# Fifteen added TensorE products between the first modulation units, and h's last low part on VectorE

## The chip, the cores and the metric

The kernel runs on one core of a Trainium2 chip. The metric is the device time of one execution in microseconds. The core has five engines, each with its own queue of instructions in a fixed order: TensorE (PE; PEld is its loading of the stationary operand), VectorE (DVE), ScalarE (ACT), GpSimd (POOL) and SyncE (SP), whose queue issues most of the transfers. The engines wait for one another through semaphores. Products on TensorE are written to banks of PSUM, from which ScalarE or VectorE copies them out.

## The reference

One layer of a streaming encoder is computed for two groups of tokens that share the weights: 256 tokens of a prompt and 8 sequences of 16 tokens. Cut to the part that the change touches:

```python
mod = silu(c) @ w_ada + b_ada            # per sequence, 6 x 1024 columns
sh1, sc1, g1, sh2, sc2, g2 = split(mod, 6)
h = rmsnorm(x, norm1_w) * (1 + sc1) + sh1
P = h @ w_in                             # RWKV-7 | sparse attention and indexer | two gates
```

After that come an RWKV-7 branch, a sparse attention branch, a gated mix with a residual, a second modulated norm and PEER, a mixture of 16,384 single-row experts of which each token picks 8 x 16. Everything is float32; a product has to keep nearly float32 accuracy.

## The kernel before

**High and low parts.** Most products are not made in float32 directly. A tile is split into a high part (`hi`, a copy in the type float32r, made on ScalarE by `hilo`, L230) and a low part (`lo = src - hi`, made on VectorE or GpSimd, L234), and hi*hi + hi*lo + lo*hi are added up in one bank. For weights these parts are `wh` and `wl`; for h they are `LTh` and `LTl`, each of 128 partitions x 8 chunks x 384 tokens (columns 0 to 127 are the sample tokens, 128 to 383 the prompt's).

**The front.** `front_x` loads x in three tiles of 128 tokens, norms them and transposes them on TensorE into `xT` (the `fx` rows). `front_h` then goes over the eight chunks of h in four steps of two, c = 0, 2, 4, 6. Step c calls `mod_unit` for unit c // 2 (shift) and unit c // 2 + 4 (scale), and turns two chunks of `xT` into h and its two parts. The high part of the samples is made on ScalarE (L485) and that of the prompt on VectorE (L486); the low part of the samples on VectorE (L487, 128 x 256), that of the prompt on GpSimd (L488, 128 x 512).

**A modulation unit** has 256 columns of `w_ada`. Its weights come in two slices of 512 KB, each into one of the four buffers `w` of the pool `stream`, from which the weights of `w_in` come too; a transfer waits until the buffer it takes has been read. A slice makes four float32 products, 32 rows x 256 columns, side by side in the array's four column groups (`mm<-w,cst`). After both slices ScalarE copies the bank (`mr`, L392), two small products with `sel` transpose it and add up its four parts (`bx<-cfirst,mr`), and VectorE adds the bias (`scT`, L397). From `scT` comes `h1A` (L404).

**What follows** is `w_in` by units of columns: wa, wb, wg (RWKV's low-rank inputs), two gate units, the indexer, and then, by the string ORDER, RWKV pairs, attention quarters, gate units and the remaining modulation units in turn. The product of a unit with h runs over h's eight chunks in `tposp` or `natp` and lands in one of two banks `mm`; ScalarE copies it out (`pt`, L502 and L503).

**What sets the order.** Within an engine the instructions don't stand as the program's text has them: a scheduler simulates a timeline with its own costs and fills each queue. An edit at one place can therefore move rows of all later stages. `d<-zero` rows clear scratch in memory, `rt` rows on GpSimd make the rotary tables (L343 to L352), `expb` and `ob` are constants of later stages; all three stand among the front's rows. The bank tag `dx` has two buffers, which stages behind the front use.

Of the kernel before, what the change touches and what calls it, by code (L numbers as in the profile page):

```python
# [18 lines left out]
OP = mybir.AluOpType  # L19
# [8 lines left out]
NT = 384  # L28
# [167 lines left out]
class K:  # L196
# [186 lines left out]
    def mod_unit(self, u):  # L383

        nc = self.nc
        p = self.ps([128, 256], tag="mm")
        for h in range(2):
            w = self.raw(self.I["w_ada"][:, u, h * 4:h * 4 + 4])
            for g in range(4):
                self.mm(p[32 * g:32 * g + 32], self.st[:, h * 4 + g], w[:, g], start=(h == 0), stop=(h == 1), tp=(0, 32 * g))  # L390
        mr = self.t([128, 256], tag="mr", bufs=2, pool=self.fill)
        nc.scalar.activation(mr, p, AF.Copy)  # L392
        if u < 8:
            q = self.ps([128, 2, 9], tag="bx")
            for c in range(2):
                self.mm(q[:, c], mr[:, c * 128:(c + 1) * 128], self.c["sel"])
            nc.vector.tensor_tensor(self.scT[:, u // 4, (u % 4) * 2:(u % 4) * 2 + 2], q,  # L397
                                    self.bcol[:, 2 * u:2 * u + 2].unsqueeze(2).to_broadcast([128, 2, 9]), op=OP.add)
        else:
            nc.sync.dma_start(self.modd[:, u * 256:(u + 1) * 256], mr)  # L400
# [62 lines left out]
    def front_h(self):  # L463

        nc = self.nc
        hi = self.t([128, 8, NT], F32R, tag="LTh", pool=self.hpool)
        lo = self.t([128, 8, NT], F32R, tag="LTl", pool=self.hpool)
        self.LT = (hi, lo)
        self.h1B = self.scT[:, 0]
        self.h1A = self.pool.tile([128, 8, 9], F32, name="h1A")  # L470
        h = self.xT
        for c in range(0, 8, 2):
            cs = slice(c, c + 2)
            self.mod_unit(c // 2)
            self.mod_unit(c // 2 + 4)
            self.mod_cols(cs)
            hs = h[:, cs, 0:128]
            o = hs.rearrange("p c (b t) -> p c b t", t=16)
            bc = lambda a: a[:, cs, :8].unsqueeze(3).to_broadcast([128, 2, 8, 16])
            nc.vector.tensor_tensor(o, o, bc(self.h1A), op=OP.mult)  # L480
            nc.vector.tensor_tensor(o, o, bc(self.h1B), op=OP.add)
            for cc in (c, c + 1):
                hp = h[:, cc, 128:NT]
                nc.scalar.activation(hp, hp, AF.Identity, scale=self.h1A[:, cc, 8:9], bias=self.h1B[:, cc, 8:9])
            nc.scalar.activation(hi[:, cs, 0:128], hs, AF.Copy)  # L485
            nc.vector.tensor_copy(hi[:, cs, 128:NT], h[:, cs, 128:NT])  # L486
            nc.vector.tensor_tensor(lo[:, cs, 0:128], hs, hi[:, cs, 0:128], op=OP.subtract)  # L487
            nc.gpsimd.tensor_tensor(lo[:, cs, 128:NT], h[:, cs, 128:NT], hi[:, cs, 128:NT], op=OP.subtract)  # L488


    def shifted(self, name, ch, tag, bufs=2):
# [1263 lines left out]
```

## Time and profile before

| | us |
|---|---|
| three runs: lowest, median, highest | 1762.54, 1763.51, 1766.21 |
| the profiled execution, whole | 1759.49 |
| its span, first to last instruction | 1757.7 |
| busy in the span: PE, DVE, ACT, POOL | 1679.5, 1353.6, 747.5, 550.5 |
| mean granted TensorE clock | 0.981 |

All rows shown below come from the profiled execution, in microseconds from the start of its span. A row of the timeline reads: start, length, engine, line, operation, what is written <- what is read, shapes, how many of them, and in brackets the idle time before it and what ended it. A row of the waits reads: who waited for whom, us in total, how often, the longest. A group's row ends with busy time, mean ns of one, and idle time before. SPq is the queue of SyncE that issues transfers. Ends of products on TensorE are modelled, and products overlap, so that the spacing of two starts says more than a length.

### The profile page before, as it was taken

The page shows a single profiled execution, that of the slowest core. Times are in us where ns is not written, and L with a number is a line of the kernel's source. Part 1 is how long each engine was busy: PE and PEld are TensorE (multiplying, and loading weights), DVE is VectorE, ACT ScalarE, POOL GpSimd, SP SyncE. Part 2 cuts the span into 40 slices and gives each one's busy share as a digit, 9 for nine tenths or more (in the row PEclk, how much of TensorE's full clock was granted, in tenths as well). Part 3 has the DMA queues.
Part 4 walks back from the last instruction along what each step waited for, and adds up shares of the span by engine and source line. Part 5 has one row for each costly group of instructions (what it writes and reads, how often), then busy time and mean ns, then how long its engine had stood idle before and what let it go on. Part 6 is the DMA issues. An engine that isn't in the chain of part 4 may idle for free.

```text
span 1757.7 us, 33129 instructions
## 1 busy us (share of the span) xinstructions
PE 1679.5 (96%) x12392; PEld 1410.2 (80%) x12392; DVE 1353.6 (77%) x2907; ACT 747.5 (43%) x1666; POOL 550.5 (31%) x616
## 2 busy tenths in 40 slices
PE   6999899999999999999998999999999999999998
PEld 4988788777888877899887889999976667767766
DVE  4448878778867765556999998899957778778787
ACT  4533343334342333335323255578853433443344
POOL 2433343333333421024032233342243224323232
PEclk8999899999999999999999999999999999999999
DMA  8543662555365365765488999997569999999996
GB/s 305 161 123 101 187 194 68 145 166 174 94 197 161 94 207 189 246 193 171 144 334 313 358 333 366 397 340 238 179 251 381 348 346 376 375 349 391 349 379 216
DMA packets 172537, 436.71 MB, mean 248 GB/s; under 512 B 46036, under 2 KB 86100, under 8 KB 155992
## 3 DMA queue, kind: packets, MB, share of 16 engines
q1 hardware_dynamic: 153944, 300.36, 50.8%
q0 software_dynamic: 18432, 134.23, 19.7%
q8 instruction: 98, 1.61, 0.4%
q14 instruction: 63, 0.52, 0.1%
HBM read 403.23 MB, written 31.30 MB: 247 GB/s over the span
## 4 chain that ended last, share of the span: by engine, by line
PE 55%; DVE 19%; DMA 11%; issue 8%; ACT 3%; POOL 2%; SPq 1%; DVEq 0%; POOLq 0%; ACTq 0%
PE mm L226 21%; PE fx L226 10%; PE dx L226 10%; PE cp L226 6%; PE bx L226 6%; DMA raw<-in_puv,pe 3%; DVE wl L234 3%; DVE raw L1580 2%; DVE acc L1586 2%; DMA w<-in_puT 2%; DMA w<-in_pv 2%; ACT wh L230 1%; DMA w<-in_w_in 1%; DVE TX L698 1%; DMA NL<-d 1%
## 5 line engine op out<-in xcount | busy, mean ns | idle before, releaser
L234 DVE TENSOR_TENSOR wl<-w,wh 128x1024 fp32r<-128x1024 f32 (+1 forms) x276 | 345.8, 1260 | 109.0 <-ACT wh L230 71.3
L230 ACT ACTIVATE wh<-w 128x1024 fp32r<-128x1024 f32 (+1 forms) x284 | 296.6, 1050 | 163.7 <-PE mm L226 74.3
L1573 POOL DMA_INDIRECT raw<-in_puv,pe x128 | 173.6, 1356 | 423.4 <-PE dx L226 155.4
L226 PE MATMUL fx<-h2h,wl 128*128 128x256 f32 x704 | 200.1, 285 | 8.2 <-DVE wl L234 8.0
L226 PE MATMUL fx<-h2h,wh 128*128 128x256 f32 x704 | 200.6, 285 | 1.4 <-ACT wh L230 1.1
L226 PE MATMUL fx<-h2l,wh 128*128 128x256 f32 x704 | 197.4, 281 | 0.0
L1586 DVE SCALAR_TENSOR_TENSOR acc<-raw,dots,acc 128x1024 f32<-128x1024 f32 x127 | 166.1, 1308 | 14.8 <-ACT dots L1582 14.8
L1580 DVE SCALAR_TENSOR_TENSOR raw<-raw,sh 128x1024 f32<-128x1024 f32 x128 | 158.9, 1241 | 14.0 <-DMA raw<-in_puv,pe 13.8
L226 PEld LDWEIGHTS fx<-h2h,wl 128*128 128x128 f32 x704 | 132.7, 189 | 12.3 <-DVE wl L234 11.5
L226 PEld LDWEIGHTS fx<-h2h,wh 128*128 128x128 f32 x704 | 132.6, 188 | 6.4 <-ACT wh L230 3.6
L226 PEld LDWEIGHTS fx<-h2l,wh 128*128 128x128 f32 x704 | 132.9, 189 | 1.6 <-issue 1.1
L226 PE MATMUL mm<-LTh,wh 128*128 128x384 f32 (+2 forms) x352 | 123.4, 351 | 1.4 <-ACT wh L230 0.8
L226 PE MATMUL mm<-LTl,wh 128*128 128x384 f32 (+2 forms) x352 | 123.1, 350 | 0.9 <-POOL LTl L488 0.9
L226 PE MATMUL mm<-LTh,wl 128*128 128x384 f32 (+2 forms) x352 | 122.4, 348 | 0.0
L226 PE MATMUL mm<-h2f,w 128*128 128x256 f32 x448 | 104.0, 385 | 0.0
L226 PE MATMUL mm<-wh,LTh 128*128 128x256 f32 x336 | 100.3, 299 | 2.9 <-ACT qx L888 2.9
L1581 ACT ACTIVATE dots<-dots 128x1 f32<-128x1 f32 x128 | 25.6, 200 | 177.0 <-DVE raw L1580 176.5
L226 PE MATMUL mm<-wl,LTh 128*128 128x256 f32 x336 | 99.4, 296 | 0.0
L226 PE MATMUL mm<-wh,LTl 128*128 128x256 f32 x336 | 98.6, 293 | 0.0
L226 PEld LDWEIGHTS mm<-h2f,w 128*128 128x128 f32 x448 | 85.0, 192 | 12.2 <-issue 0.2
L226 PE MATMUL fx<-h2f,w 128*128 128x256 f32 x320 | 73.8, 383 | 0.0
L226 PEld LDWEIGHTS mm<-LTh,wh 128*128 128x128 f32 (+2 forms) x352 | 66.5, 189 | 7.1 <-issue 3.0
(577 smaller groups left out, 4235.0 us busy)
## 6 DMA issues: line engine op xcount, KB each, us to landing
w<-in_puT SPq DMA_DIRECT2D x128, 512.0 KB, 7.1
w<-in_pv SPq DMA_DIRECT2D x128, 512.0 KB, 6.6
w<-in_w_in SPq DMA_DIRECT2D x70, 512.0 KB, 4.5
w<-in_w_ada SPq DMA_DIRECT2D x48, 512.0 KB, 4.8
cKT<-in_cKT SPq DMA_DIRECT2D x32, 256.0 KB, 4.3
cV<-in_cV SPq DMA_DIRECT2D x32, 256.0 KB, 4.5
w<-in_w_pq SPq DMA_DIRECT2D x16, 512.0 KB, 4.2
d<-wst SPq DMA_DIRECT2D x8, 832.0 KB, 4.3
```

Of the source, the lines that this page charges most:

```text
L226: return self.nc.tensor.matmul(out, l, r, start=start, stop=stop, skip_group_check=True, **kw)
L230: self.nc.scalar.activation(hi, src, AF.Copy)
L234: (self.nc.vector if eng == "v" else self.nc.gpsimd).tensor_tensor(lo, src, hi, op=OP.subtract)
L698: nc.vector.tensor_tensor(X[:, :t, :t], T[:, :t, :t].rearrange("p s c -> p c s"), NL[:, :t, t].unsqueeze(1).to_broadcast([48, t, t]), op=O ...
L1573: d = nc.gpsimd.indirect_dma_start(out=bass.AP(tensor=u.tensor, offset=u.offset, ap=[u.ap[0], [1, 2048]]), out_offset=None, in_=self.I["puv"],
L1580: nc.vector.scalar_tensor_tensor(u, u, 1.0, h2, op0=OP.mult, op1=OP.mult, accum_out=dot)
L1581: nc.scalar.activation(dot, dot, AF.Gelu_apprx_tanh)
L1586: nc.vector.scalar_tensor_tensor(acc, v, dot, acc, op0=OP.mult, op1=OP.add)
```

## The change

Behind the four products of a slice, in units 0 to 7, TensorE makes one more product: the identity as stationary operand times the slice's last quarter (128 x 128 by 128 x 256, float32), into a bank `wake` that nothing reads. The last slice of unit 7 is left out, so there are fifteen. The bank is one of the two `dx` buffers, taken once ahead of the loop. In the last step (c = 6) the prompt's low part is made on VectorE and no more on GpSimd.

```diff
--- before.py
+++ after.py
@@ -388,6 +388,8 @@
             w = self.raw(self.I["w_ada"][:, u, h * 4:h * 4 + 4])
             for g in range(4):
                 self.mm(p[32 * g:32 * g + 32], self.st[:, h * 4 + g], w[:, g], start=(h == 0), stop=(h == 1), tp=(0, 32 * g))
+            if u < 8 and (u, h) != (7, 1):
+                self.mm(self.wake, self.ident, w[:, 3])
         mr = self.t([128, 256], tag="mr", bufs=2, pool=self.fill)
         nc.scalar.activation(mr, p, AF.Copy)
         if u < 8:
@@ -469,6 +471,7 @@
         self.h1B = self.scT[:, 0]
         self.h1A = self.pool.tile([128, 8, 9], F32, name="h1A")
         h = self.xT
+        self.wake = self.ps([128, 256], tag="dx")
         for c in range(0, 8, 2):
             cs = slice(c, c + 2)
             self.mod_unit(c // 2)
@@ -485,7 +488,7 @@
             nc.scalar.activation(hi[:, cs, 0:128], hs, AF.Copy)
             nc.vector.tensor_copy(hi[:, cs, 128:NT], h[:, cs, 128:NT])
             nc.vector.tensor_tensor(lo[:, cs, 0:128], hs, hi[:, cs, 0:128], op=OP.subtract)
-            nc.gpsimd.tensor_tensor(lo[:, cs, 128:NT], h[:, cs, 128:NT], hi[:, cs, 128:NT], op=OP.subtract)
+            (nc.vector if c == 6 else nc.gpsimd).tensor_tensor(lo[:, cs, 128:NT], h[:, cs, 128:NT], hi[:, cs, 128:NT], op=OP.subtract)
 
 
     def shifted(self, name, ch, tag, bufs=2):
```

The lines of the changed kernel are two or three further down from there on. How the queues stand now is shown at three places; a number behind a name tells one buffer of a tile from another, and such numbers differ between the two programs throughout.

TensorE, the first two units. `mm` are the products of a slice, `dx` the added ones, `fx` transposes of the second x tile, `bx` the sel products. Before:

```order
L226 MATMUL mm_174<-w_175,cst 32x256 x4
L226 MATMUL mm_174<-w_181,cst 32x256 x4
L460 MATMUL fx_138<-cfirst,xn_131 128x128 x4
L460 MATMUL fx_144<-cfirst,xn_131 128x128 x4
L226 MATMUL mm_193<-w_194,cst 32x256 x4
L226 MATMUL bx_189<-cfirst,mr_187 128x9 x2
L226 MATMUL mm_193<-w_200,cst 32x256 x4
L226 MATMUL mm_221<-w_222,cst 32x256 x4
```

And with the change:

```order
L226 MATMUL mm_175<-w_176,cst 32x256 x4
L226 MATMUL dx_174<-w_176,cfirst 128x256
L226 MATMUL mm_175<-w_183,cst 32x256 x4
L226 MATMUL dx_174<-w_183,cfirst 128x256
L462 MATMUL fx_138<-cfirst,xn_131 128x128 x4
L462 MATMUL fx_144<-cfirst,xn_131 128x128 x4
L226 MATMUL mm_196<-w_197,cst 32x256 x4
L226 MATMUL dx_174<-w_197,cfirst 128x256
L226 MATMUL mm_196<-w_204,cst 32x256 x3
L226 MATMUL bx_192<-cfirst,mr_190 128x9 x2
L226 MATMUL mm_196<-w_204,cst 32x256
L226 MATMUL dx_174<-w_204,cfirst 128x256
```

Each slice `w` is now read by a fifth product that stands directly behind its four; the transposes of the second x tile stand behind two of these.

VectorE, at the end of the front. `wl` are low parts of the weights of wa (128x1024), wb (128x1024) and wg (128x768); `bx_349` before and `bx_365` after are the sel products of unit 7, the last. Before:

```order
L234 TENSOR_TENSOR wl_419<-w_362,wh_418 128x1024
L234 TENSOR_TENSOR wl_460<-w_364,wh_459 128x1024
L397 TENSOR_TENSOR scT<-bx_349,bcol 128x18
L234 TENSOR_TENSOR wl_501<-w_366,wh_500 128x768
L332 TENSOR_TENSOR expb<-cfront 128x512
L1058 TENSOR_SCALAR ob_349_1810<-cfront 128x8
L404 SCALAR_TENSOR_TENSOR h1A<-scT,cols 128x18
L480 TENSOR_TENSOR xT_107<-xT_107,h1A 128x2x128
L481 TENSOR_TENSOR xT_107<-xT_107,scT 128x2x128
L486 CAST LTh_171<-xT_107 128x2x256
L487 TENSOR_TENSOR LTl_172<-xT_107,LTh_171 128x2x128
```

And with the change:

```order
L399 TENSOR_TENSOR scT<-bx_365,bcol 128x18
L406 SCALAR_TENSOR_TENSOR h1A<-scT,cols 128x18
L483 TENSOR_TENSOR xT_107<-xT_107,h1A 128x2x128
L234 TENSOR_TENSOR wl_435<-w_378,wh_434 128x1024
L484 TENSOR_TENSOR xT_107<-xT_107,scT 128x2x128
L489 CAST LTh_171<-xT_107 128x2x256
L234 TENSOR_TENSOR wl_476<-w_380,wh_475 128x1024
L491 TENSOR_TENSOR LTl_172<-xT_107,LTh_171 128x2x256
L234 TENSOR_TENSOR wl_517<-w_382,wh_516 128x768
L332 TENSOR_TENSOR expb<-cfront 128x512
L1061 TENSOR_SCALAR ob_350_1826<-cfront 128x8
L490 TENSOR_TENSOR LTl_172<-xT_107,LTh_171 128x2x128
```

The rows of unit 7 and the first step on xT now stand ahead of the weights' low parts, and the prompt's low part of h (128x2x256) is among the rows, ahead of `wl` of wg; the samples' one (128x2x128) is now behind `wl` of wg, `expb` and `ob`.

ScalarE, the same place. `wh` are the high parts of wa, wb, wg and of the two gate units that follow (the last two of them); `mr_347` before and `mr_363` after are the copy of unit 7's bank; `pt` is the copy out of wa's bank. Before:

```order
L230 ACTIVATE wh_418<-w_362 128x1024
L392 ACTIVATE mr_347<-mm_334 128x256
L230 ACTIVATE wh_459<-w_364 128x1024
L230 ACTIVATE wh_500<-w_366 128x768
L484 ACTIVATE xT_107<-xT_107,scT,h1A 128x256 x2
L485 ACTIVATE LTh_171<-xT_107 128x2x128
L230 ACTIVATE wh_555<-w_553 128x1024
L230 ACTIVATE wh_590<-w_588 128x1024
L502 ACTIVATE pt_422<-mm_426 128x8x16
L503 ACTIVATE pt_422<-mm_426 128x256
```

And with the change:

```order
L394 ACTIVATE mr_363<-mm_349 128x256
L230 ACTIVATE wh_434<-w_378 128x1024
L487 ACTIVATE xT_107<-xT_107,scT,h1A 128x256 x2
L230 ACTIVATE wh_475<-w_380 128x1024
L230 ACTIVATE wh_516<-w_382 128x768
L488 ACTIVATE LTh_171<-xT_107 128x2x128
L230 ACTIVATE wh_571<-w_569 128x1024
L230 ACTIVATE wh_606<-w_604 128x1024
L505 ACTIVATE pt_438<-mm_442 128x8x16
L506 ACTIVATE pt_438<-mm_442 128x256
```

The copy of unit 7 moved ahead of the split of wa's weights, and xT of the last two chunks ahead of the splits of wb and wg; the two splits ahead of wa's `pt` stand where they stood.

On GpSimd the one row of the prompt's last low part, which stood behind the rotary tables, is gone. SyncE's queue has the same rows in the same order up to the attention stage. On TensorE the rows behind the front stand in the same order until the first attention quarter, apart from a few among wa's and wb's; from there on to the end of the RWKV and attention stages the rows of all engines stand in another order in some hundreds of small places, and in PEER again almost as before.

## The prediction, made before the changed kernel ran

> **What bounds the kernel now.** I read the page's busy rows first, then the first 60 us by stretches, then each engine's rows there in order of time, last the waits of the DMA queue.
>
> ```profile
> span 1757.7 us, 33129 instructions
> ...
> PE 1679.5 (96%) x12392; PEld 1410.2 (80%) x12392; DVE 1353.6 (77%) x2907; ACT 747.5 (43%) x1666; POOL 550.5 (31%) x616
> ```
>
> TensorE is busy for 96% of the span, so time is to be won in what it waits for and in the rate at which it works. Both are poor at the start. The windows below give, by stretch, the length, then busy us (and rows) of PE, PEld, DVE, ACT and POOL, the granted clock, the share of the DMA engines and GB/s.
>
> ```profile
> 8.00:12.00 4.00, 2.58 (x16) 1.97 (x20) 1.57 (x3) 2.18 (x4) 1.14 (x2) 1.00 1.03 407
> ...
> 16.00:20.00 4.00, 3.54 (x44) 2.03 (x41) 2.19 (x7) 2.03 (x6) 0.55 (x1) 1.00 0.99 343
> 20.00:24.00 4.00, 2.59 (x32) 1.36 (x24) 1.58 (x6) 2.16 (x6) 1.38 (x1) 1.00 0.92 324
> ...
> 28.00:32.00 4.00, 4.00 (x30) 1.96 (x30) 0.89 (x4) 0.74 (x2) 0.00 (x0) 0.50 0.94 323
> ...
> 41.50:44.00 2.50, 2.50 (x16) 2.50 (x15) 0.81 (x3) 0.56 (x2) 2.50 (x7) 0.96 0.69 144
> 44.00:48.00 4.00, 3.13 (x18) 2.81 (x17) 0.10 (x2) 1.27 (x2) 3.69 (x11) 1.00 1.01 401
> ```
>
> The granted clock is 1.00 up to 24 us, 0.50 in the stretch from 28, and 0.96 after 41.5. The DMA share is 0.92 or more up to 32 us: here the transfers set the pace as well. Next, TensorE's own rows.
>
> ```profile
> 19.18 1.07 PE L226 MATMUL mm<-w,cst 128*32 128x256 f32 x16
> ...
> 24.95 1.08 PE L226 MATMUL mm<-w,cst 128*32 128x256 f32 x8 [1.13 <-DMA w<-in_w_ada]
> 26.32 1.08 PE L226 MATMUL mm<-w,cst 128*32 128x256 f32 x8 [0.29 <-DMA w<-in_w_ada]
> ...
> 28.29 1.94 PE L226 MATMUL mm<-w,cst 128*32 128x256 f32 x16
> ...
> 34.05 1.08 PE L226 MATMUL mm<-w,cst 128*32 128x256 f32 x8
> ...
> 38.84 0.52 PE L226 MATMUL mm<-LTh,wh 128*128 128x384 f32 x1
> 39.16 0.52 PE L226 MATMUL mm<-LTl,wh 128*128 128x384 f32 x1
> ...
> 44.49 0.34 PE L226 MATMUL mm<-LTl,wh 128*128 128x384 f32 x1
> 44.66 0.34 PE L226 MATMUL mm<-LTh,wl 128*128 128x384 f32 x1
> ...
> 46.74 0.44 PE L226 MATMUL mm<-LTl,wh 128*128 128x384 f32 x1 [0.87 <-POOL LTl L488]
> ...
> 49.34 0.41 PE L226 MATMUL mm<-LTh,wh 128*96 128x384 f32 x1 [0.59 <-ACT pt L503]
> ```
>
> A slice of modulation weights (one half unit, four products, eight rows) takes 0.53 us at 19 us and 0.94 to 0.97 at 28 us. The row at 26.32 is the last one that waits for a slice: from there on TensorE itself, at half clock, is the slower side. The products of wa and wb step by 0.32 us at 38.84 and by 0.17 at 44.49. Then two waits stand on the path: 0.87 us for h's last low part (until 46.74) and 0.59 us for ScalarE to empty wa's bank, before wg can start at **49.34**. From there TensorE hardly stops:
>
> ```profile
> 50.00:100.00 50.00, 49.93 (x339) 47.29 (x338) 26.36 (x33) 23.94 (x44) 23.56 (x35) 1.00 0.48 144
> 183.00:800.00 617.00, 594.21 (x6146) 508.31 (x6146) 446.06 (x1106) 229.00 (x518) 187.70 (x262) 0.98 0.54 166
> ```
>
> 49.93 of 50 us are busy from 50 to 100, so the start of wg is the mark to watch: what moves it moves what follows by as much, as long as nothing else falls behind.
>
> **The change, step by step.** *The price of one added product.* None like it (128 columns of identity, 256 of weights) is in the trace, but the PEER products have its form:
>
> ```profile
> L226 PE MATMUL mm<-h2f,w 128*128 128x256 f32 x448 | 104.0, 385 | 0.0
> ```
>
> 104.0 / 448 is 0.232 us a row. A float32 product makes two rows (the two slices at 19.18 are eight products, x16), so one added product is 0.46 us at full clock, and 0.93 at half (estimate, twice). Fifteen are 7.0 us of TensorE at full clock, 14 at half. They lie where TensorE waits for slices, so the first question is the transfers.
>
> *The ring of four weight buffers.*
>
> ```profile
> 12.46 17.30 SPq L240 DMA_DIRECT2D w<-in_w_ada  x12
> ```
> ```profile
> SPq L240 <- PE mm L226: 16.0, 14, 2.6
> ```
>
> Each of these twelve issues waits for TensorE to be done with a buffer, 16.0 us in all over the first 60. An added product reads the slice last, so it holds every buffer 0.46 us longer (0.93 early on). The first two releases come at half clock: the rows give 12.46 now, about 13.2 and then 14.6 for the second after the change. Bounds: the transfers lose nothing (the queue still holds three slices), or all 1.3 us. I take 0.8 us lost there, since the first delay alone is 0.7. Against that, at full clock a slice and its added product take 0.53 + 0.46 = 0.99 us, and the 0.58 us of sel products (22.67, below) fall once per two slices: 1.28 us a slice, where half clock without them takes 0.96 + 0.51 = 1.47. The tail from 26 us on is thus no longer held by TensorE: 6 x 0.19 = 1.1 us. The last slice itself, without an added product, is 0.4 shorter at full clock. Its end, 34.05 + 1.08 = 35.1 now, becomes 35.1 + 0.8 - 1.1 - 0.4 = **34.4**, with bounds 33.6 (nothing lost) and 36.0 (1.3 lost, no gain in the tail).
>
> *Whether the clock holds.* From 16 to 20 us TensorE was busy for 3.54 of 4.0 us (88%) and kept full clock; from 20 to 24, with 2.59 (65%) and no longer pause than the 1.13 us before 24.95, it lost it. With the added products it is busy for 1.28 us of every 1.4 to 1.6 in which a slice comes, 80 to 91%: nearer the stretch that held. I take it as held, and price the other as a rival, since the row of 28 to 32 us, 4.00 of 4.00 busy at 0.50, shows that busy time alone doesn't settle it.
> The Trainium skill's page "TensorE: Matmul & The Clock Gate" (Part 1, "What's actually happening") says that the clock falls only after a whole idle window of some 3.4 us, and rises after one busy window of that length. By that rule the added products could not fail, and the rival below would have no chance. This trace disagrees: the fall came after pauses of 1.13 us at most, and four busy microseconds (28 to 32) did not raise it, so the rival stays.
>
> *From the last slice to a complete h.* The rows that price the steps:
>
> ```profile
> 22.67 0.58 PE L226 MATMUL bx<-cfirst,mr 128*128 128x9 f32 x4 [0.36 <-DVE scT L397]
> ```
> ```profile
> 34.79 1.06 ACT L230 ACTIVATE wh<-w 128x1024 fp32r<-128x1024 f32 x1 [1.48 <-DMA w<-in_w_in]
> 35.75 0.37 ACT L392 ACTIVATE mr<-mm 128x256 f32<-128x256 f32 x1
> ...
> 40.66 1.09 ACT L484 ACTIVATE xT<-xT,scT,h1A 128x256 f32<-128x256 f32 x2 [1.99 <-DVE h1A L404]
> ```
> ```profile
> 35.88 2.50 DVE L234 TENSOR_TENSOR wl<-w,wh 128x1024 fp32r<-128x1024 f32 x2 [0.98 <-ACT wh L230]
> ...
> 39.77 0.69 DVE L332 TENSOR_TENSOR expb<-cfront 128x512 bf16<-128x512 f32 x1
> ...
> 40.45 0.17 DVE L404 SCALAR_TENSOR_TENSOR h1A<-scT,cols 128x18 f32<-128x18 f32 x1
> ...
> 42.13 0.42 DVE L487 TENSOR_TENSOR LTl<-xT,LTh 128x256 fp32r<-128x256 f32 x1
> ```
> ```profile
> 42.64 2.82 POOL L352 TENSOR_TENSOR rt<-rt,qkn 128x96 f32<-128x96 f32 x8
> 45.42 1.26 POOL L488 TENSOR_TENSOR LTl<-xT,LTh 128x512 fp32r<-128x512 f32 x1
> ```
>
> Before, the copy of the last unit stood behind a weight split on ScalarE, the next step behind two low parts on VectorE, and the last low part behind the 2.82 us of rope products on GpSimd, so that h was whole at 45.42 + 1.26 = 46.7. In the new order: copy 34.4 to 34.8, sel products to 35.4, scT and h1A (0.2 each) to 35.8, xT (0.43) to 36.2; ScalarE splits wa's weights from 34.8 to 35.9, then does xT to 37.0, wb to 38.05, wg to 38.9, LTh to 39.3. VectorE: wl of wa 36.2 to 37.4, xT 37.85, LTh (after ScalarE's xT) 38.3, wl of wb 39.5, the moved low part 40.2, wl of wg 41.2, expb 41.9, ob, the last LTl 42.5. The moved step, 128x512 on VectorE, has no row; it lies between the 0.42 of 128x256 and the 1.25 of 128x1024, and I take the 0.69 of expb, which has its size. h is whole at **42.5**, 4.2 us earlier. After the last LTl VectorE now stands idle until 46.75, so the 0.69 us hide there; if that cover went, wl of wg would come 0.69 late, and it is not needed before 45.
>
> *TensorE on wa and wb.* It starts at 35.9 as before, and its third row waits for wl of wa, 37.4. The 46 rows left at 0.174 end at 45.4; wa's own last row, the 43rd, at 44.5. No row of these then waits for h. Even if the idle time before 37.3 costs the clock again for one stretch, ten rows at 0.15 more make wa's end 46.0. Taken alone 3.3 us are won (49.34 - 0.59 = 48.75 to 45.4).
>
> *What is late next.* wg needs wa's bank, and ScalarE empties it behind two weight splits, in the new order as in the old:
>
> ```profile
> 39.77 1.09 SPq L365 DMA_DIRECT2D d<-zero  x2
> 40.95 2.69 SPq L240 DMA_DIRECT2D w<-in_w_in  x4
> ```
> ```profile
> SPq L365 <- DMA cfront<-in_cfront: 1.5, 1, 1.5
> ```
> ```profile
> 45.62 1.06 ACT L230 ACTIVATE wh<-w 128x1024 fp32r<-128x1024 f32 x1 [3.56 <-DMA w<-in_w_in]
> 47.78 1.06 ACT L230 ACTIVATE wh<-w 128x1024 fp32r<-128x1024 f32 x1 [1.11 <-PE mm L226]
> ...
> 48.91 0.38 ACT L503 ACTIVATE pt<-mm 128x256 f32<-128x256 f32 x1
> ```
>
> The first split waits until 45.62 for a transfer that is issued at 40.95, right behind two writes held until the constants have landed (39.77). None of that hangs on h. The second split waited for TensorE; now it waits for its own transfer, which is 0.5 MB behind the first, at 400 GB/s about 1.3 us, 46.9 (estimate from the 44-to-48 rate of the same trace). 46.9 + 0.96 + 0.64 for the two copies is **48.5** for wg, against 49.34. Three quarters of the 3.3 us are given back to a transfer.
>
> Sum: 0.8 us less. The profiled execution took 1759.49, 1.8 beyond its span; the three runs' median is 4.0 higher. Taking the difference to the median: 1763.5 - 0.8 = **1762.7**. With the ends (transfers a microsecond earlier, which the tail could give; or 1.6 later, the last slice at 36.0) wg starts between 47.5 and 50.1: this case spans 1761.7 to 1764.3, and with as much as the median's own spread below, 1 us (1762.54 to 1766.21), 1760.7 to 1764.3.
>
> **The rivals.** *The gain arrives whole.* Where a freed ring brings the transfers 2 to 3 us forward, ScalarE is not held and wg starts one copy (0.64) after wa's 44.5, but not before wb is done, at 45.7: 3.6 us won, 1759.9. For: 16 to 32 us moved 323 to 343 GB/s, 8 to 12 us 407. Against: the DMA share was 0.92 or more in all of these.
> *The clock falls all the same* (the slower side). From 24.95 six more slices carry an added product of 0.93 us on a TensorE that has no slack: 5.6 us, and the last slice ends at 40.7. The third row of wa follows 3.0 us later as above and 0.4 more for sel products at half clock, 44.1; 46 rows, 10 of them at 0.32, take 9.5; wg starts at 53.6, 4.3 us late: 1767.8. Without any row at 0.32 it would be 1766.3. It decides at one point: whether the clock is 1.0 or 0.5 after about 24 us.
> *The rest of the schedule.* Behind the front, TensorE's rows stand in the old order for a while (by their place in it up to some 183 us of the old trace), then in another one up to some 800, in the alternation of RWKV pairs and attention quarters; VectorE's differ from 36 us on. TensorE idles 617.0 - 594.2 = 22.8 us there (row above). If a quarter of these waits goes or comes, 5.7 us, the time is 1757.0 or 1768.4. Nothing in the profile says which.
> *The change does not do what it says* (nobody waits for the moved part, products finish in slack already): that is 1763.5, and is inside the first case.
>
> **How the numbers follow.** The front alone 0.42; whole gain 0.12; clock falls 0.14; later order for the better 0.19, for the worse 0.13. A measurement of this kernel tells 0.2%, 3.5 us, from no change: under 1760.0 is faster, over 1767.0 slower. Faster: 0.19 + 0.09 of the whole gain + 0.05 of the first case's edge = 0.33. Slower: 0.13 + 0.10 of the fallen clock = 0.23. Same: 0.44. The range 1755.5 to 1769.0 takes in all cases but the outer parts of the later order.
>
> **What would show it.** Right: granted clock 1.0 from some 14 us to past 35; slices near 1.4 us apart; the last low part on VectorE ending near 42; then a wait of TensorE for ScalarE's copy, with the weight split ahead of that copy waiting for its transfer; wg near 48.5. Wrong: clock 0.5 in 24 to 41; issues of slices later by more than 1.3 us; wg near 45.7; or idle time of TensorE from 183 to 800 us more than 2 us away from 22.8.

## The result, and the profile after

| | before | after |
|---|---|---|
| median of six runs each, us | 1763.43 | 1784.06 |
| lowest and highest, us | 1760.62, 1770.69 | 1776.11, 1789.32 |
| profiled execution, whole; its span, us | 1759.49; 1757.7 | 1777.51; 1775.7 |
| mean granted TensorE clock | 0.981 | 0.987 |

The ratio is 1.0101, with a 95% interval of 1.0076 to 1.0127: the change makes the kernel slower by 1%, 18 to 21 us, with a clock that is higher than before. First the page of the changed kernel, span and busy rows:

```profile
span 1775.7 us, 33168 instructions
...
PE 1688.8 (95%) x12422; PEld 1412.1 (80%) x12422; DVE 1357.0 (76%) x2908; ACT 749.1 (42%) x1666; POOL 542.8 (31%) x615
```

TensorE has 30 products and 30 weight loads more (15 float32 products of two rows each) and is busy for 9.3 us more, of which about 8 can be the added products (0.54 us each, below). The span grew by 18. The stretches at the start, in the columns of the prediction's windows, first one of before that the prediction does not show, then the changed kernel's:

```profile
12.00:16.00 4.00, 4.00 (x36) 2.42 (x32) 0.01 (x1) 2.07 (x5) 0.00 (x0) 1.00 0.94 333
```
```profile
12.00:16.00 4.00, 4.00 (x25) 1.71 (x18) 0.00 (x0) 0.81 (x2) 0.00 (x0) 1.00 0.65 186
16.00:20.00 4.00, 4.00 (x30) 1.92 (x28) 1.08 (x3) 2.50 (x5) 0.55 (x1) 1.00 0.80 244
20.00:24.00 4.00, 4.00 (x41) 2.45 (x40) 1.21 (x4) 1.85 (x4) 0.00 (x0) 1.00 0.83 264
...
28.00:32.00 4.00, 3.97 (x38) 2.23 (x37) 3.03 (x6) 1.68 (x5) 1.27 (x1) 1.00 0.92 319
...
40.00:44.00 4.00, 2.60 (x9) 2.29 (x10) 3.93 (x8) 2.92 (x5) 0.00 (x0) 0.81 0.88 279
44.00:48.00 4.00, 4.00 (x19) 4.00 (x19) 2.40 (x5) 0.67 (x2) 2.30 (x7) 0.76 0.94 273
```

The clock is 1.00 where it was 0.50 (28 to 32 us): the added products do hold it while there are slices. Behind them it falls after all, 0.81 and 0.76 in the last two rows, on the products of wa and wb. (The records of the clock begin at 15.2 us in this trace and at 14.4 in before's, so the 1.00 of earlier windows is not measured: the first slice, at 11.72, still takes 1.01 us.) And the transfers are starved: 186 GB/s and then 244 in the two stretches from 12 us, where before has 333 and 343. The queue of SyncE and the engines' rows say why, and where it leads:

```profile
SPq L240 <- PE dx L226: 17.7, 11, 3.7
...
SPq L240 <- PE bx L226: 5.4, 4, 1.5
```
```profile
20.00 0.64 PE L226 MATMUL mm<-w,cst 128*32 128x256 f32 x8
20.57 0.70 PE L226 MATMUL dx<-w,cfirst 128*128 128x256 f32 x2
21.11 0.51 PE L226 MATMUL bx<-cfirst,mr 128*128 128x9 f32 x4
...
38.12 0.64 PE L226 MATMUL mm<-w,cst 128*32 128x256 f32 x8
```
```profile
43.68 0.69 DVE L491 TENSOR_TENSOR LTl<-xT,LTh 128x512 fp32r<-128x512 f32 x1
...
45.84 1.96 SPq L240 DMA_DIRECT2D w<-in_w_in  x4
46.02 0.41 DVE L490 TENSOR_TENSOR LTl<-xT,LTh 128x256 fp32r<-128x256 f32 x1
...
50.37 1.06 ACT L230 ACTIVATE wh<-w 128x1024 fp32r<-128x1024 f32 x1 [5.71 <-DMA w<-in_w_in]
...
52.83 0.38 ACT L506 ACTIVATE pt<-mm 128x256 f32<-128x256 f32 x1
...
53.27 0.42 PE L226 MATMUL mm<-LTh,wh 128*96 128x384 f32 x1 [1.44 <-ACT pt L506]
```

Before, the issues waited for TensorE for 16.0 us in all, behind the slices' own products (the prediction's row). Now it is 17.7 us behind added products, eleven times, and 5.4 behind sel products, four times. The last slice ends at 38.12 + 0.64 = 38.8, where it ended at 35.1; the next issue of `w_in` stands at 45.84 and no more at 40.95, ScalarE waits 5.71 us for it, and wg starts at 53.27: 3.9 us late. The transfer is not alone in this: ScalarE's second split waits for TensorE once more, 0.28 us until 51.71, and ten products of wa and wb had stepped by 0.32 us in place of 0.17 there, from 42.75 on, at the fallen clock (before, twelve had). These 3.9 us are the smaller part of the loss. Where the rest comes from, I read from both traces row by row: the difference of start times of the same VectorE and ScalarE rows, median by stretches of before's time.

```
before's time, us    75-175  225-275  375-425  525-575  725-825  1200-1300  end
after                  3.9     0.2      5.3     15.0     12.1      14.8    18.0
```

The front's 3.9 us are even won back for a while, then 15 us are lost between 225 and 575, in the RWKV and attention stage, and some 6 behind 825, in PEER.

### The profile page after: what moved, and what is told of

It reads as the page before. It is cut to its first block, busy times and chain, and to the rows that moved or that the text cites. A ratio compares the mean times of both kernels' runs of the same rounds, so it can differ in the third digit from the quotient of the medians.

```text
span 1775.7 us, 33168 instructions
## 1 busy us (share of the span) xinstructions
PE 1688.8 (95%) x12422; PEld 1412.1 (80%) x12422; DVE 1357.0 (76%) x2908; ACT 749.1 (42%) x1666; POOL 542.8 (31%) x615
## 4 chain that ended last, share of the span: by engine, by line
PE 38%; DVE 16%; DMA 14%; issue 7%; ACT 3%; POOL 2%; SPq 0%; DVEq 0%; POOLq 0%; ACTq 0%
PE mm L226 13%; PE fx L226 9%; PE dx L226 6%; PE cp L226 5%; DMA raw<-in_puv,pe 5%; PE bx L226 4%; DMA w<-in_pv 4%; DVE wl L234 3%; DVE raw L1583 2%; DMA w<-in_puT 2%; DVE acc L1589 2%; ACT wh L230 2%; DVE TX L701 1%; POOL raw L1576 1%; DVE psi L1318 1%
```

## The experiments

Four theories were tried one after the other; the second and the third were formed on what the runs before them showed. Each kernel ran in several rounds beside before on the same chip. Ratios are to before, with 95% intervals.

### One part of the change at a time

`r1_lo_only`: before with the last line of the diff alone. `r2_wake_only`: the change without that line.

```diff
-            nc.gpsimd.tensor_tensor(lo[:, cs, 128:NT], ...
+            (nc.vector if c == 6 else nc.gpsimd).tensor_tensor(lo[:, cs, 128:NT], ...
```

> The last low part on VectorE alone, no added products; from the first attention quarter on the rows stand in a third order, neither the old one nor that of the change. Front: the part costs 0.69 us on VectorE where it stands idle, so wg starts within 1 us of the old 49.3 us. Theory 'ring plus order' (the added products hold the weight buffers, +3.9 us at wg; the later order adds some 8 us up to the start of PEER, 842 us before): what this kernel differs from before comes from the order alone, so the stretch from wg to PEER's first product changes by some us in either direction while the front doesn't. Rival 'the added products alone cost' : within 0.2% of before, 1760 to 1767 us.

> The fifteen added products as in the change, the last low part on GpSimd again; a fourth order of the later rows. Theory 'ring plus order': the slices come as late as in the change, wg starts at 52 to 54 us, and the rest from wg to PEER is another draw, in -3 to +9 us. Rival 'the added products alone cost': all of the 18 us of the changed kernel's profile stay, 1776 to 1789 us. Rival 'the low part's move is what costs': 1760 to 1767 us.

Measured: r1 1759.95 us, 0.9983 (0.9965 to 1.0002); r2 1771.71 us, 1.0050 (1.0028 to 1.0073). Neither alone has the loss of both together.

`r3_wake_const`: the added products read the identity (128 columns) and not the slice, so that they hold no buffer; they are also half as long. `r4_wake_quarter`: they read 64 columns of the slice in place of 256; low part on GpSimd.

```diff
-                self.mm(self.wake, self.ident, w[:, 3])
+                self.after(self.mm(self.wake[:, :128], self.ident, self.ident[:, :128]), m)   # r3, m: the slice's last product
+                self.mm(self.wake[:, :64], self.ident, w[:, 3, :64])                          # r4
```

> The added products read the identity in place of the slice (128 columns, half as long), each behind its slice's last product, so that they hold no weight buffer; the low part on VectorE. The rows behind the front stand in exactly the order of the changed kernel. Theory 'ring plus order': the transfers run as before (DMA share over 0.9 from 12 to 24 us), wg starts at 48 to 50 us, at most 0.7 us later than before, and the loss from wg to the start of PEER, 8 us in the changed kernel's profile, stays whole: 1768 to 1780 us. Rival 'all of it comes from the front' (late transfers shift the stages against each other): it is gone, 1760 to 1767 us.

> The added products read 64 of the 256 columns, low part on GpSimd; the rows behind the front stand in exactly the order of the kernel before. Theory 'ring plus order': a buffer is held 0.12 us longer at full clock, 0.23 at half, a quarter of before; the first two issues are some 0.3 and 0.5 us late; wg starts within 1.5 us of 49.3; the total within 0.2% of before, 1760 to 1767 us. Rival 'the added products alone cost, by their number': slower by a good part of the 18 us.

Measured: r3 1780.78 us, 1.0097 (1.0072 to 1.0121); r4 1783.05 us, 1.0112 (1.0084 to 1.0139). Windows of r3 and its wg row:

```profile
12.00:16.00 4.00, 4.00 (x36) 2.08 (x29) 0.00 (x0) 1.44 (x5) 0.00 (x0) 1.00 0.86 262
16.00:20.00 4.00, 4.00 (x42) 2.86 (x46) 1.88 (x7) 1.92 (x5) 0.55 (x1) 1.00 0.86 293
20.00:24.00 4.00, 3.35 (x34) 1.76 (x34) 1.17 (x3) 2.61 (x7) 1.38 (x1) 1.00 0.99 347
```
```profile
50.53 0.42 PE L226 MATMUL mm<-LTh,wh 128*96 128x384 f32 x1 [0.59 <-ACT pt L508]
```

Without the hold on the slices the transfers run at 262 to 347 GB/s and wg starts 1.2 us late in place of 3.9, with the clock at 1.00: this speaks for the held buffers as most of the front's loss. r3 came out a little worse than I expected of it: a DMA share of 0.86 where I had asked for over 0.9, and wg 0.5 us and the time 0.8 us over their ranges. One execution is little for this, so I read all of them: in the nine traces with products on most slices wg starts at 52.4 to 58.4 us, 53.3 in the median, in the eleven others (r5 and r8, with a single one, among them) at 48.2 to 53.5, 50.5 in the median. By these medians the hold costs some 2.8 us, though the two sets overlap. Their length alone does not explain it: the products of r12 (below), of 32 columns, hold buffers too, and wg starts at 52.37 there. But r3 is nearly as slow as the change, so the front isn't the main cause. r4 missed by 20 us what I expected of it, though all its later rows stand in before's order, row for row.

### Does the bank of the added tile matter?

The tile `wake` takes one of the two `dx` banks, so every later `dx` tile stands in the other one. r5 and r8 take the bank with a single product of one column, in before and in r1; r6 and r7 give r4 and the change a second such tile, which puts the later tiles back.

```diff
+        self.wake2 = self.ps([128, 256], tag="dx")      # r6, r7, with one product of one column into it
```

> Before, with the unread tile and a single product of 1 column into it (after slice 0 of unit 0); every other row and its order as before. The tile takes one of the two banks of the tag dx, so that every later tile of that tag stands in the other bank. Theory A (the bank that later dx tiles get costs the time): 10 to 20 us slower, 1773 to 1783, with the growth between 80 and 825 us and in the last stage as in the quarter wakes. Theory B (the added rows of the first stage cost it: transfers starved at the start and what follows): within 2 us of before, 1761 to 1765.

> The quarter wakes of r4 (64 columns of each slice), and a second unread dx tile with one product of 1 column, so that later dx tiles stand in the banks that they had before. Order of the later rows as before. Theory A (banks): the 12 to 21 us of r4 go but for the front's 3.7: 1762 to 1768. Theory B (rows of the first stage): as r4, 1778 to 1788.

> The change as it is, and a second unread dx tile with one product of 1 column, so that later dx tiles stand in the banks that they had before; order of the later rows as in the change. Theory A (banks): the later loss of about 14 us goes and the front's 3.9 stays: 1764 to 1770. Theory B (the starved transfers of the first stage) and theory C (the later order that the scheduler made of the change): as the change, 1776 to 1789.

> The low part on VectorE alone (r1, 1759.95), and the unread tile with one product of 1 column, so that later dx tiles change banks; order of the later rows as in r1. Theory A (banks): 10 to 20 us slower than r1, 1770 to 1780. Theory B (rows of the first stage): as r1, 1757 to 1764.

Measured: r5 1.0007 (0.9984 to 1.0030), r8 1.0004 (0.9984 to 1.0025), r6 1.0097 (1.0061 to 1.0133), r7 1.0100 (1.0068 to 1.0132). Theory A (the bank) has fallen in all four: the bank costs nothing that these runs could tell, and r6 and r7 keep the loss with the old banks. What the slow kernels have in common is more than a few added products.

### Does the place in TensorE's instruction stream matter?

The page counts how instructions reach the engines. The queue's row has packets, MB, and share; here of before, and of r14 (below), which has 256 TensorE rows more:

```profile
q8 instruction: 98, 1.61, 0.4%
```
```profile
q8 instruction: 99, 1.62, 0.4%
```

Each packet is 16,384 bytes, and in before's trace one comes per 255.4 rows of TensorE (products and weight loads): a block of 256 rows of 64 bytes. Added rows move all that follows to other places in these blocks. r9, r10, r14 and r15 add 15, 32, 64 and 79 products of 1 x 1 ahead of all work, where TensorE is idle until 9.4 us (32 take 1.7 us there); each product is four rows. r11 is r4 with so many of them (49) that 256 rows are added in all. r12 is r4 with 32 columns.

```diff
+        self.wake = self.ps([128, 256], tag="dx")
+        for _ in range(N):                              # 15, 32, 49, 64 or 79
+            self.mm(self.wake[:1, :1], self.ident[:, :1], self.ident[:, :1])
```

> Before, with 15 unread products of 1 row by 1 column (identity by identity) ahead of the first transpose, in the 9.4 us in which TensorE has nothing to do: as many rows of TensorE as the change adds (30 weight loads and 30 products), none of them beside the slices. Theory F (the added rows move all that follows in TensorE's instruction stream, which is fetched in 98 blocks of 16.4 KB, to worse places in the blocks): 10 to 20 us slower, 1773 to 1783. Theory G (the products must stand among the slices, in time or data, to cost): within 3 us of before, 1760 to 1766.

> The same with 32 products ahead, 128 added rows. Theory F: another shift, so another time; anything from before's to 20 us slower. Theory G: within 3 us of before, 1760 to 1766.

> The quarter wakes of r4 and 49 products of 1 row by 1 column ahead of the first transpose, so that 64 products and 256 rows are added in all, the 16.4 KB of one block at 64 bytes a row. Theory F: what follows the first stage stands in its blocks as before, and r4's later loss goes: 1763 to 1769 (the front's 3.7 us stay). Theory G: as r4 and r6, 1776 to 1786.

> Wakes of 32 columns in place of 64 or 256; low part on GpSimd; order of the later rows as before. Theory F (rows count, not columns): as r4, 1776 to 1786. Theory G with time as what costs (a product of 32 columns takes little more than its weight loads, 0.2 us against r4's 0.24 to 0.25 and the change's 0.46): half of r4's loss or less, 1765 to 1774. Theory H (each product holds its slice's buffer and starves the transfers, however short it is): as r4.

> Before, with 64 products of 1 row by 1 column ahead of the first transpose: 256 rows, one block. Theory F with blocks of 256 rows: as before, 1761 to 1766. Theory K (the more rows are added, the slower, or rows at the start cost in another way): r9's 1773 or more.

> The same with 79 products: 316 rows, one block and the 60 rows of r9. Theory F with blocks of 256 rows: as r9, 1769 to 1778. Theory L (r9 was chance, and rows ahead do nothing): as before, 1761 to 1766.

Measured, all with later rows in before's order:

| | rows added | ahead of all work | among the slices |
|---|---|---|---|
| r5 | 4 | | 1.0007 (0.9984 to 1.0030) |
| r10 | 128 | 0.9979 (0.9957 to 1.0001) | |
| r14 | 256 | 1.0005 (0.9983 to 1.0027) | |
| r9 | 60 | 1.0049 (1.0025 to 1.0072) | |
| r15 | 256 + 60 | 1.0069 (1.0049 to 1.0090) | |
| r12, r4, r6 | 60, 60, 64 | | 1.0078, 1.0112, 1.0097 |
| r11 | 256 | | 1.0020 (0.9997 to 1.0042) |

Fifteen products of no size, in time that was idle, cost 0.5% and 79 of them 0.7%, while 32 and 64 cost nothing that can be told. The loss of 60 rows comes back at 316, 256 further on, the size of a block; these few places don't exclude a shorter period. r11 takes most of r4's loss away by adding rows. So r4, r6 and r12 are slow mostly for the number of rows added, as place in the blocks would have it, and the rest fits the front within the intervals: in their traces wg starts at 52.4 to 53.3, 3.0 to 4.0 us late, which is 0.2%.

How the block's place costs time stays open. That the blocks are the reason is argued from the 256 rows and not shown. TensorE does not stop at the fetch: in before's trace it idles 2.7% of the time in the 2 us after a fetch starts, and 3.9% on average behind 20 us. The loss lies in waits elsewhere: r9's span is 8.5 us longer than before's (1766.2), and TensorE is busy for only 1.0 us more (1680.5). One example, the same product in before and in r9 (start, length, idle time before):

```profile
1319.82 0.28 PE L226 MATMUL fx<-h2h,wh 128*128 128x256 f32 x1
```
```profile
1327.07 0.38 PE L226 MATMUL fx<-h2h,wh 128*128 128x256 f32 x1 [1.39 <-ACT wh L230]
```

The step to this product from the one before it is 0.23 us in before, r5, r11 and r10, 0.53 in r6, but 1.78 to 1.94 in r9, r4 and r12, and 1.38 in r15. The blocks are not all of it: r13 and r18 (below), at 256 rows, have 1.03 and 2.06 here. Whether the packet delays a transfer of data or something else, no run tells.

### Is it the block in the change itself?

`r13_change_block` gives the change 49 products ahead, 256 rows in all; `r16_lo_32_ahead` tries r1 at r10's place.

> The change as it is, and 49 products of 1 row by 1 column ahead of the first transpose: 64 products and 256 rows added in all, one block of 16,384 bytes. Theory F (the 60 rows that the change adds move what follows to other places in the blocks in which TensorE's instructions are fetched): the front's 3.9 us stay and the rest of the change's 18 to 20 us goes: 1765 to 1770. Theory C (the later order that the scheduler made of the change costs it): as the change, 1777 to 1785. Both in part: between, 1770 to 1777.

> The low part on VectorE alone (r1), with the 32 products of r10 ahead (128 rows). If the gains of r1 (0.17%) and r10 (0.21%) are each real and add up: 1755 to 1758. If the place in the blocks that suits before's order does not suit r1's: 1759 to 1768.

Measured: r13 1781.72 us, 1.0111 (1.0087 to 1.0135); r16 1760.03 us, 0.9989 (0.9972 to 1.0006). Theory F (the place in the blocks), which fits before's order, does not explain the change: r13 is as slow as the change at 60 rows and r7 at 64. The two small gains don't add up either; none of r1, r10 and r16 can be told from before, so no version here beats it.

### The order that the scheduler makes

`r17_order_alone` has no product on a slice and the low part on GpSimd: 8 products of the identity by itself behind unit 3's slices tip the scheduler into the change's later order, row for row on all four engines from some 67 us on, and 56 ahead fill up the 256 rows. `r18_change_other_order` is the change with 4 such products and 45 ahead: its later order is another one, near to r1's.

```diff
+            if u == 3:
+                for _ in range(4):                      # r18: 2
+                    self.after(self.mm(self.wake[:, :128], self.ident, self.ident[:, :128]), m)
```

> Before (low part on GpSimd, no product reads a slice), with 8 unread products of the identity by itself, 128 columns each, behind unit 3's slices, and 56 of 1 row by 1 column ahead: 256 rows in all, so that the rest stands in its blocks as before. These few products make the scheduler put all later rows in the order of the change, row for row. Theory C (that order costs the time in the change): 10 to 15 us slower than before, 1773 to 1778, the growth between 225 and 575 us. Theory M (the order is as good as before's, and the products on the slices or what they delay cost it): 1763 to 1767.

> The change as it is (15 products on the slices, low part on VectorE), with 4 more products of 128 columns behind unit 3's slices and 45 of 1 row by 1 column ahead (256 rows in all): the scheduler's later order is then another one, near to that of r1. Theory C: the loss of the change but the front's 4 us goes, 1764 to 1770. Theory M: as the change, 1777 to 1785.

Measured: r17 1781.08 us, 1.0093 (1.0069 to 1.0118); r18 1777.58 us, 1.0066 (1.0046 to 1.0086). With the change's later order, no product on a slice and before's place in the blocks, the loss is the change's within the intervals (3 us more than I had expected). It is not quite the later order alone: in r17's trace wg starts at 52.94, 3.6 us late, so its front is no better than the change's. r3 covers that side: its wg starts at 50.53, only 1.2 us late, and its ratio is 1.0097 all the same. r18 missed: its loss is two thirds of the change's, so the order it got isn't free; that it is near to r1's does not make it as good.

The traces show the order's price at one place. As above, the median shift against before's trace, us, for one execution each:

```
before's time, us    75-175  225-275  375-425  525-575  725-825  1200-1300  end
the change's order
after (60 rows)        3.9     0.2      5.3     15.0     12.1      14.8    18.0
r3    (60)             1.2    -1.1      4.2     13.7     12.9      11.7    16.5
r7    (64)             3.2     2.7      7.1     18.1     15.5      15.2    22.1
r13   (256)            6.9     5.1     12.4     20.8     19.6      20.9    25.7
r17   (256)            3.8     6.0     11.9     21.2     19.5      19.9    25.2
before's order
r5    (4)              0.1     0.7      2.1      1.8      0.0       0.2    -0.5
r14   (256)            2.6     6.1      5.6      5.7      3.5       5.7     9.3
r9    (60)             0.7     1.1      2.1      5.1      5.3       4.7     8.5
other orders
r1    (0)              1.2     0.0      1.1      1.8     -0.5      -0.9    -2.5
r18   (256)            4.5     3.4      9.2     12.8     10.6      10.4    18.8
```

All five with the change's order grow by 14.8 to 15.7 us between 225-275 and 525-575 and give 1 to 3 back; with before's order it is -0.4 to 4.0 in the three shown, and some -2.6 to 4.6 in the other six. (Of these r4, r12 and r15, with 60 or 316 rows, lose more later on: by 725-825 they have grown by 7.5 to 10. At 256 rows, r13 and r17 have grown by 13 to 15 there and r14 and r11 by under 1.) Waits are only a part of it. The stretch from before's 183 to 800 us, at the times that the shifts give for the change and for r17 (length, then busy us and rows of PE, PEld, DVE, ACT, POOL, clock, DMA):

```profile
187.00:812.00 625.00, 598.83 (x6143) 509.82 (x6142) 444.67 (x1105) 229.62 (x517) 181.15 (x262) 0.98 0.53 164
```
```profile
186.80:819.50 632.70, 605.93 (x6148) 513.88 (x6148) 444.31 (x1106) 228.91 (x518) 181.93 (x262) 0.97 0.53 162
```

TensorE's idle time is 26.2 and 26.8 us against 22.8 before, 3.4 to 4.0 more, while the stretch is 8 and 15.7 us longer. The rest is busy time for the same count of rows (6146 before). The clock does not explain it in the changed kernel, whose row has before's 0.98. Some products overlap less in this sequence. The 128 products that read `ev`, each 268 ns long in the median in all these traces, cover this, before and after (length, then busy us of these products alone):

```profile
183.00:800.00 617.00, 6.88 (x128) 0.98 0.54 166
```
```profile
187.00:812.00 625.00, 8.69 (x128) 0.98 0.53 164
```

It is 8.60 to 8.96 in r3, r13 and r17, and 7.12 in r14, over the same work. Other groups lose or gain a microsecond or two likewise, and none makes up the whole. The largest single wait that grew is TensorE's for ScalarE's `qx`, here of before and of after:

```profile
PE mm L226 <- ACT qx L888: 1.9, 1, 1.9
```
```profile
PE mm L226 <- ACT qx L891: 4.3, 2, 2.8
```

Which of the many places in the order make the loss was not tried.

## Why the prediction was wrong, point by point

*The clock* ("I take it as held"): right for the stretch it was said of. It is 1.00 from 28 to 32 us, as shown, and 1.00 from 24 to 32 in r2 as well. With 64 columns it fell, as r4's windows show:

```profile
20.00:24.00 4.00, 3.51 (x37) 2.00 (x37) 0.94 (x3) 2.00 (x6) 1.38 (x1) 1.00 0.98 366
24.00:28.00 4.00, 3.19 (x26) 1.70 (x26) 2.88 (x6) 1.71 (x4) 1.27 (x1) 0.74 0.92 336
28.00:32.00 4.00, 4.00 (x28) 2.75 (x27) 0.69 (x4) 0.38 (x1) 0.00 (x0) 0.50 0.85 272
```

The Trainium skill's page "TensorE: Matmul & The Clock Gate" (Part 1, "What's actually happening") lets the clock fall only after a whole idle window; r4 fell in a stretch with 3.19 of 4 us busy, so here too the trace disagrees. The prediction's own measure, the busy share, does not settle it either: r3 kept its clock with less.

```profile
24.00:28.00 4.00, 2.96 (x33) 1.56 (x33) 2.17 (x7) 1.67 (x4) 0.43 (x1) 1.00 0.95 301
```

What the clock was worth is the other half: nothing that shows. r3 holds it without holding slices, and its last slice ends at 35.4, where before's ended at 35.1 at half clock: the faster TensorE did not bring it forward. Then r3's clock falls too, and the half clock lands on wa and wb as it did before: fifteen of their products step by 0.32 us, where twelve did in before and ten do in the changed kernel. wg starts at 50.53, not before 49.34. What a clock held through wa and wb would give, no run tells.

*The price of an added product* (0.46 us at full clock): mis-sized a little; 20.57 to 21.11 is 0.54, and 0.63 where the next slice's products are behind it (37.49 to 38.12).

*The ring of four weight buffers* ("I take 0.8 us lost there", bounds 0 to 1.3; the tail wins 1.1): this step of the front failed. The mechanism was named, but priced at two releases of the first buffers. It acts on eleven, since each added product stands in TensorE's queue between a slice and its release, and the waits for TensorE add up to 23.1 us (17.7 and 5.4) where they were 16.0. The last slice ended at 38.8, not at 34.4 (bounds 33.6 to 36.0).

*The moved low part* (0.69 us, from a row of its size): measured 0.69. *h whole at 42.5*: 46.4, since all of it hangs on the last slice.

*What is late next*: the place was right, ScalarE's split ahead of wa's copy waiting for a transfer issued behind held writes, and a late front moves that issue too (45.84). wg is at 53.27, 3.9 us late. The ten products that the prediction allowed to fall to half clock here did so (42.75 to 45.63). With this size right the sum would have been 1767.4, slower by 0.2%.

*The rest of the schedule* ("If a quarter of these waits goes or comes, 5.7 us"): here the prediction lost most. The rival stood in the text with the right sign at 0.13, but its price was bounded by TensorE's idle time, 22.8 us, on the thought that a busy engine can lose only through waits. In the traces the change's order costs 13 to 15 us there, with 3.4 more of idle time. r17 shows this order, at before's place in the blocks and with no product on a slice, at 1.0093 where the change has 1.0101 (its front 3.6 us late), and r3 at 1.0097 with a front only 1.2 us late. My "what would show it" asked for an idle time more than 2 us off, and it was 3.4 off; that mark would have told the sign and not the size.

*Missing altogether*: that 60 added rows move all that follows in TensorE's instruction stream. With before's order 60 and 316 rows cost 0.5 and 0.7%, for a reason that stays open. With the change's order no run shows a price (256, 60 and 64 rows: 1.0111, 1.0101, 1.0100), so nothing of this result is put down to it. Nor is the growth behind 825 us in after's trace, 5.9 us: r14, whose median is before's, grows by 5.8 there in its profiled execution, so one trace can't tell it from chance.

## What to carry to other kernels

An added read of a streamed tile is priced by how long it keeps the buffer from the queue of transfers, over the whole run of tiles, and not by its own length. Where a scheduler orders the program, a small edit in the first stage can buy another order of every later stage; bound that by what orders differ by when tried (here 1%), not by the idle time, and try the order by itself before crediting or blaming the edit. An experiment that adds rows to a full engine should be repeated with other numbers of rows, a whole instruction block among them, before its last half per cent is believed.

## What the runs showed of the hardware that was not expected

TensorE's instructions are fetched while the kernel runs, 98 packets of 16,384 bytes, one per 255.4 rows. Fifteen and 79 products of 1 x 1 in idle time made the kernel 0.49 and 0.69% slower (60 and 316 rows), while 32 and 64 gave 0.9979 and 1.0005. The granted clock was held through a stage that waits for transfers by added products of 256 columns, and of 128 in r3; with 64 columns it fell. The busy share of 4 us does not tell these apart: it was 2.96 of 4 where r3 held, and 3.51 and then 3.19 where r4 fell. And the same 128 products, of the same length each, covered 6.9 us in one order of the rows and 8.6 to 9.0 in another.
